# Batched A·Bᵀ on one core: ScalarE and VectorE put into hardware loops, transposes of a and b taken in turn, GpSimd counting landed loads

## The chip, the cores and the metric

One core of one Trainium2 chip. The metric is the device time of one execution in microseconds (us); several executions are taken, and the profiled execution gives the trace. All runs compared here are of the fast state unless a sentence says otherwise. A ratio is the mean time of one kernel's fast runs over the mean time of the other's fast runs in the same rounds, so it is not quite the ratio of the medians quoted next to it. PE is TensorE, DVE is VectorE, ACT is ScalarE, POOL is GpSimd, SP is SyncE.

## The reference

```python
batch, m, k, n = 16, 512, 512, 512          # a: (16,512,512) f32, b: (16,512,512) f32
def reference(a, b):
    return np.matmul(a, b.transpose(0, 2, 1)).astype(np.float32)
```

That is 33.55 MB to read and 16.78 MB to write.

## The kernel before

The 16 products are done as 8 pairs. For each pair SyncE loads 2 MB of a and 2 MB of b; VectorE casts them to bf16 in two halves of the columns (`ha`, `wa`, `hb`, `wb`); PE transposes `ha` and `hb` into PSUM (groups 0 and 1), VectorE copies `wa` over `ha` and `wb` over `hb`, PE transposes those (groups 2 and 3). ScalarE evicts the transposed a to `ta`, VectorE the transposed b to `tb`. Then PE runs 32 matmuls into four PSUM banks, ScalarE copies each result to `ob`, and stores of 1 MB leave. Seven buffers hold loads, seven hold outputs. I call the time from the first transpose of a pair to its first matmul a **turn**, and the 32 matmuls a **block**.

```python
ORDER = "LLLLLLLSLLLLSLSSLSLSLLSSSSSSSSS"     # SyncE: loads and stores; store 0 goes from ScalarE
...
for u in range(pairs):                         # VectorE, unrolled
    ...                                        # casts of a and b, each after its own load
    for ko in range(KO):
        if ko < 2:
            h, w, s_c, s_t = both[ko]
            nc.vector.wait_ge(s_cd, 2 * u + ko + 1)
            nc.vector.wait_ge(s_t, KO * u + 2)
            nc.vector.tensor_copy(out=h[:], in_=w[:]).then_inc(s_c, 1)
        nc.vector.wait_ge(s_tb, KO * u + ko + 1)
        nc.vector.tensor_copy(out=tb[:, ko, :], in_=tp[:, 2 + ko % 2]...).then_inc(s_eb, 1)
...
for x, (h, s_c, s_t, s_e) in enumerate(...):   # PE: a, then b
    take(s_c, 1)
    for g in range(2):
        take(s_e, 1)
        for j in range(2 * J):
            t = nc.tensor.transpose(tp[:, 2 * x + g, j, :], h[:, j, g * P:(g + 1) * P], ident[:])
        t.then_inc(s_t, 1)
```

PE was in a hardware loop already. The waits in its loop have constant counts, while the totals grow with the pair, so there a wait is a `take`: wait for n, then subtract n. In the profile a take is an instruction of the engine's sequencer (51 ns on PE; after the change 21 ns on VectorE and 17 ns on ScalarE); PEq, DVEq or ACTq with the take's line (L186 before, L136 after) as the end of an idle time means that the take was what came last.

Of the kernel before, what the change touches and what calls it, by code (L numbers as in the profile page):

```python
# [10 lines left out]
def kernel(  # L11
# [6 lines left out]
    nc = tc.nc  # L18
    P = 128
    batch, M, K = a.shape  # L20
    _, N, _ = b.shape
    J = M // P
    KO = K // P
    HP = P // 2
    HK = K // 2
    pairs = batch // 2
    f32 = mybir.dt.float32
    bf16 = mybir.dt.bfloat16
    NL = 7
    NO = 7  # L30


    ORDER = "LLLLLLLSLLLLSLSSLSLSLLSSSSSSSSS"

    def sbuf(name, shape, dtype):
        return ctx.enter_context(nc.sbuf_tensor(name, shape, dtype))

    def sem(name):
        return tc.alloc_semaphore(name)

    with tc.tile_critical(no_gpsimd_drain=True):  # L41
        ident = sbuf("ident", [P, P], bf16)
        ld = [sbuf(f"ld{i}", [P, 2 * J, K], f32) for i in range(NL)]
        ha, wa, hb, wb = (
            sbuf(name, [P, 2 * J, HK], bf16) for name in ("ha", "wa", "hb", "wb")
        )
        ta = sbuf("ta", [P, KO, 2 * J * P], bf16)
        tb = sbuf("tb", [P, KO, 2 * J * P], bf16)
        ob = [sbuf(f"ob{i}", [P, J, N], f32) for i in range(NO)]
        tp = ctx.enter_context(nc.psum_tensor("tp", [P, 4, 2 * J, P], bf16))  # L50
        ps = ctx.enter_context(nc.psum_tensor("ps", [P, 4, N], f32))

# [1 line left out]
        s_ld = [sem(f"s_ld{i}") for i in range(NL)]  # L54
        s_second = [sem(f"s_second{i}") for i in range(2)]
        s_st = [sem(f"s_st{i}") for i in range(NO)]
        s_cd = sem("s_cd")
        s_ca = sem("s_ca")
        s_cb = sem("s_cb")
        s_ta = sem("s_ta")  # L60
        s_tb = sem("s_tb")
        s_ea = sem("s_ea")
        s_eb = sem("s_eb")
        s_mm = sem("s_mm")
        s_pv = sem("s_pv")
        s_out = sem("s_out")
# [10 lines left out]



        n_ld, n_st = 0, 1  # L80
        for what in ORDER:
            if what == "L":
                u, slot = n_ld // 2, n_ld % NL
                src = (a if n_ld % 2 == 0 else b)[2 * u:2 * u + 2].rearrange(
                    "e (p j) k -> (e p) j k", j=2 * J
                )
                if n_ld >= NL:

                    nc.sync.wait_ge(s_cd, n_ld - NL + 1)
                if n_ld < 2:  # L90
                    nc.sync.dma_start(
                        ld[slot][:, :J, :], src[:, :J, :]
                    ).then_inc(s_ld[slot], 16)
                    nc.sync.dma_start(
                        ld[slot][:, J:, :], src[:, J:, :]
                    ).then_inc(s_second[slot], 16)
                else:
                    nc.sync.dma_start(ld[slot][:], src).then_inc(s_ld[slot], 16)
                n_ld += 1
            else:  # L100
                slot = n_st % NO
                nc.sync.wait_ge(s_out, n_st + 1)
                nc.sync.dma_start(
                    out[n_st].rearrange("(p j) n -> p j n", j=J), ob[slot][:]
                ).then_inc(s_st[slot], 16)
                n_st += 1
        for n in range(batch - NO, batch - 1):
            nc.sync.wait_ge(s_st[n % NO], 16 * (n // NO + 1))




        nc.vector.nop().then_inc(s_eb, 2)
        nc.vector.wait_ge(s_set, 2)
        both = ((ha, wa, s_ca, s_ta), (hb, wb, s_cb, s_tb))
        for u in range(pairs):
            for x, (h, w, s_c, s_t) in enumerate(both):
                n = 2 * u + x
                src = ld[n % NL]
                nc.vector.wait_ge(s_ld[n % NL], 16 * (n // NL + 1))  # L120
                nc.vector.wait_ge(s_t, KO * u)
                if n >= 2:
                    nc.vector.tensor_copy(out=h[:], in_=src[:, :, :HK]).then_inc(s_c, 1)  # L123
                    nc.vector.tensor_copy(out=w[:], in_=src[:, :, HK:]).then_inc(s_cd, 1)  # L124
                else:
                    nc.vector.tensor_copy(out=h[:, :J, :], in_=src[:, :J, :HK])  # L126
                    nc.vector.tensor_copy(out=w[:, :J, :], in_=src[:, :J, HK:])  # L127
                    nc.vector.wait_ge(s_second[n], 16)
                    nc.vector.tensor_copy(  # L129
                        out=h[:, J:, :], in_=src[:, J:, :HK]  # L130
                    ).then_inc(s_c, 1)
                    nc.vector.tensor_copy(  # L132
                        out=w[:, J:, :], in_=src[:, J:, HK:]
                    ).then_inc(s_cd, 1)
            for ko in range(KO):
                if ko < 2:  # L136
                    h, w, s_c, s_t = both[ko]
                    nc.vector.wait_ge(s_cd, 2 * u + ko + 1)
                    nc.vector.wait_ge(s_t, KO * u + 2)
                    nc.vector.tensor_copy(out=h[:], in_=w[:]).then_inc(s_c, 1)  # L140
                nc.vector.wait_ge(s_tb, KO * u + ko + 1)
                nc.vector.tensor_copy(  # L142
                    out=tb[:, ko, :],
                    in_=tp[:, 2 + ko % 2].rearrange("k j p -> k (j p)"),
                ).then_inc(s_eb, 1)


        nc.scalar.nop().then_inc(s_ea, 2)
        for u in range(pairs):
            for ko in range(KO):  # L150

                nc.scalar.wait_ge(s_ta, KO * u + ko + 1)
                for e in range(2):
                    c = nc.scalar.copy(  # L154
                        out=ta[:, ko, e * J * P:(e + 1) * J * P].rearrange(
                            "k (j p h) -> k j p h", j=J, h=2
                        ),
                        in_=tp[:, ko % 2, :, e * HP:(e + 1) * HP].rearrange(
                            "k (h j) p -> k j p h", h=2
                        ),  # L160
                    )
                c.then_inc(s_ea, 1)
            for e in range(2):
                i = 2 * u + e
                if i >= NO:
                    nc.scalar.wait_ge(s_st[i % NO], 16 * (i // NO))
                for j in range(J):
                    nc.scalar.wait_ge(s_mm, J * i + j + 1)

                    c = nc.scalar.copy(  # L170
                        out=ob[i % NO][:, j, :].rearrange("m (p j) -> m p j", j=2 * J),
                        in_=ps[:, j, :].rearrange("m (j p) -> m p j", j=2 * J),
                    )
                    if j == J - 1:
                        c.then_inc(s_out, 1)
                    elif e == 0 or j == 0:
                        c.then_inc(s_pv, 1)
                    if i == 1 and j == 0:
                        nc.scalar.wait_ge(s_out, 1)
                        nc.scalar.dma_start(  # L180
                            out[0].rearrange("(p j) n -> p j n", j=J), ob[0][:]
                        ).then_inc(s_st[0], 16)


        def take(s, n):
            nc.tensor.wait_ge(s, n).then_inc(s, -n)  # L186

        pe = nc.tensor.engine
        with nc.Fori(0, pairs, engines=[pe]):
            with nc.Fori(0, 2, engines=[pe]):  # L190

                for x, (h, s_c, s_t, s_e) in enumerate(
                    ((ha, s_ca, s_ta, s_ea), (hb, s_cb, s_tb, s_eb))
                ):
                    take(s_c, 1)
                    for g in range(2):
                        take(s_e, 1)
                        for j in range(2 * J):
                            t = nc.tensor.transpose(  # L199
                                tp[:, 2 * x + g, j, :], h[:, j, g * P:(g + 1) * P], ident[:]  # L200
                            )
                        t.then_inc(s_t, 1)
            nc.tensor.wait_ge(s_ea, 2)
            nc.tensor.wait_ge(s_eb, 2)


            for e in range(2):
                for j in range(J):
                    if e == 1 and j % 2 == 0:
                        take(s_pv, 2)  # L210
                    for ko in range(KO):
                        t = nc.tensor.matmul(  # L212
                            ps[:, j, :],
                            ta[:, ko, (e * J + j) * P:(e * J + j + 1) * P],
                            tb[:, ko, :].rearrange("k (j p) -> k j p", j=2 * J)[
                                :, :, e * HP:(e + 1) * HP
                            ],
                            start=(ko == 0),
                            stop=(ko == KO - 1),
                        )  # L220
                    t.then_inc(s_mm, 1)
# [34 lines left out]
```

## Time and profile before

| | before |
|---|---|
| time, median of the first 3 runs | 126.25 us (126.08 to 126.59) |
| span of the profiled run | 124.3 us |
| busy share PE, DVE, ACT | 74%, 55%, 57% |
| DMA | near 100% from 3 to 120 us, mostly 420 to 450 GB/s |
| first block starts, last block starts | 20.59, 107.62 us |

The important part is how the end hangs on the last store and what slack compute has. Beside the slices and windows that the prediction shows, two rows of before matter: from the DMA view the last store's issue to landing (last column, us), and from the view of tile `ld` the range of the loads.

```profile
out_dram<-ob SPq DMA_DIRECT2D x1, 1024.0 KB, 7.6
...
DMA to landing us min/median/max: 5.1/26.0/37.5
```

The last store takes 7.6 us although it is 1 MB, because other stores stand in front of it: the one before it, issued at 111.88, takes 8.6 us itself, and after the change the last store meets an empty queue and takes 3.9 us. That queue is the slack: as long as it is not empty when the last store arrives, compute may be later at little or no cost (in order_only below the last store leaves 2.1 us later, and the ratio is 1.0016, 0.9969 to 1.0063).

### The profile page before, as it was taken

What the parts mean: (1) busy time and instruction counts of PE and PEld (TensorE: products, weight loads), DVE (VectorE), ACT (ScalarE), POOL (GpSimd) and SP (SyncE); (2) the same over time, 40 slices, a digit from 0 to 9 for tenths busy, and PEclk for the clock granted to TensorE, in tenths of its full rate; (3) what the DMA queues carried; (4) which work ended last, traced back from release to release, by engine and by line L of the source; (5) the groups of instructions that cost most, each with busy time, mean ns of one, the idle gap of its engine ahead of it and who ended that gap; (6) DMA issues with size and microseconds to landing.
All of it is one profiled execution on the core that took longest, in us unless ns stands there. A gap on an engine that the chain in (4) does not pass through costs nothing. (4 is left out here: it accounts for less than half of the span.)

```text
span 124.3 us, 2076 instructions
## 1 busy us (share of the span) xinstructions
PE 91.8 (74%) x768; PEld 56.5 (45%) x768; DVE 67.9 (55%) x84; ACT 71.0 (57%) x129; POOL 0.7 (1%) x6
## 2 busy tenths in 40 slices
PE   0005397998699869986998699869986998699000
PEld 0005394447444744574447444744474447443000
DVE  0065668827891788278907890782686568400000
ACT  4006042769476946694669476947694769476100
POOL 2000000000000000000000000000000000000000
PEclk9999999999999999999999999999999999999955
DMA  3999999999999999999999999999999999999980
GB/s 79 403 427 451 443 427 427 427 427 374 411 427 424 445 432 443 424 422 430 414 430 406 416 451 387 403 451 416 448 427 422 419 422 427 427 427 427 424 377 34
DMA packets 4898, 50.35 MB, mean 405 GB/s; under 512 B 544, under 2 KB 544, under 8 KB 544
## 3 DMA queue, kind: packets, MB, share of 16 engines
q1 hardware_dynamic: 4752, 49.29, 94.5%
q10 hardware_dynamic: 144, 1.05, 2.0%
q14 instruction: 2, 0.02, 0.0%
HBM read 33.55 MB, written 16.78 MB: 405 GB/s over the span
## 5 line engine op out<-in xcount | busy, mean ns | idle before, releaser
L212 PE MATMUL ps<-tb,ta 128*128 128x512 bf16 x256 | 57.3, 379 | 8.0 <-DVE tb L142 8.0
L170 ACT COPY ob<-ps 128x512 f32<-128x512 f32 x64 | 37.6, 587 | 30.1 <-PE ps L212 30.1
L212 PEld LDWEIGHTS ps<-tb,ta 128*128 128x128 bf16 x256 | 23.9, 97 | 39.0 <-ACT ta L154 8.2
L154 ACT COPY ta<-tp 128x512 bf16<-128x512 bf16 x64 | 32.9, 604 | 13.3 <-PE tp L199 12.9
L199 PE MATMUL tp<-ident,ha 128*128 128x128 bf16 x256 | 19.7, 230 | 11.8 <-PEq L186 10.9
L199 PEld LDWEIGHTS tp<-ident,ha 128*128 128x128 bf16 x256 | 16.7, 104 | 15.5 <-issue 13.8
L142 DVE COPY tb<-tp 128x1024 bf16<-128x1024 bf16 x32 | 21.3, 685 | 3.9 <-PE tp L199 3.6
L199 PE MATMUL tp<-ident,hb 128*128 128x128 bf16 x256 | 18.5, 230 | 3.1 <-PEq L186 3.1
L199 PEld LDWEIGHTS tp<-ident,hb 128*128 128x128 bf16 x256 | 16.3, 104 | 3.4 <-issue 3.3
L140 DVE COPY ha<-wa 128x2048 bf16<-128x2048 bf16 x8 | 5.5, 693 | 18.1 <-PE tp L199 18.1
L123 DVE CAST hb<-ld 128x2048 bf16<-128x2048 f32 x7 | 8.6, 1226 | 7.2 <-DMA ld<-in_b_dram 7.2
L123 DVE CAST ha<-ld 128x2048 bf16<-128x2048 f32 x7 | 8.5, 1219 | 0.6 <-DMA ld<-in_a_dram 0.6
L124 DVE CAST wb<-ld 128x2048 bf16<-128x2048 f32 x7 | 8.5, 1221 | 0.0
L124 DVE CAST wa<-ld 128x2048 bf16<-128x2048 f32 x7 | 8.5, 1220 | 0.0
L140 DVE COPY hb<-wb 128x2048 bf16<-128x2048 bf16 x8 | 5.5, 685 | 0.2 <-PE tp L199 0.2
L126 DVE CAST ha<-ld 128x1024 bf16<-128x1024 f32 x1 | 0.7, 694 | 6.1 <-DMA ld<-in_a_dram 6.1
L154 ACT ACT_TABLE_LOAD x1 | 1.3, 1283 | 1.0 <-SPq L41 1.0
L129 DVE CAST hb<-ld 128x1024 bf16<-128x1024 f32 x1 | 0.7, 694 | 1.2 <-DMA ld<-in_b_dram 1.2
L126 DVE CAST hb<-ld 128x1024 bf16<-128x1024 f32 x1 | 0.7, 695 | 1.2 <-DMA ld<-in_b_dram 1.2
L129 DVE CAST ha<-ld 128x1024 bf16<-128x1024 f32 x1 | 0.7, 694 | 1.1 <-DMA ld<-in_a_dram 1.1
L132 DVE CAST wa<-ld 128x1024 bf16<-128x1024 f32 x1 | 0.7, 689 | 0.0
L127 DVE CAST wa<-ld 128x1024 bf16<-128x1024 f32 x1 | 0.7, 687 | 0.0
(8 smaller groups left out, 2.3 us busy)
## 6 DMA issues: line engine op xcount, KB each, us to landing
out_dram<-ob SPq DMA_DIRECT2D x15, 1024.0 KB, 25.8
ld<-in_a_dram SPq DMA_DIRECT2D x7, 2048.0 KB, 30.8
ld<-in_b_dram SPq DMA_DIRECT2D x7, 2048.0 KB, 30.5
ld<-in_a_dram SPq DMA_DIRECT2D x2, 1024.0 KB, 6.1
ld<-in_b_dram SPq DMA_DIRECT2D x2, 1024.0 KB, 10.1
out_dram<-ob ACTq DMA_DIRECT2D x1, 1024.0 KB, 12.2
```

What stands on the lines that cost most here:

```text
L123: nc.vector.tensor_copy(out=h[:], in_=src[:, :, :HK]).then_inc(s_c, 1)
L124: nc.vector.tensor_copy(out=w[:], in_=src[:, :, HK:]).then_inc(s_cd, 1)
L126: nc.vector.tensor_copy(out=h[:, :J, :], in_=src[:, :J, :HK])
L127: nc.vector.tensor_copy(out=w[:, :J, :], in_=src[:, :J, HK:])
L129: nc.vector.tensor_copy(out=h[:, J:, :], in_=src[:, J:, :HK]).then_inc(s_c, 1)
L132: nc.vector.tensor_copy(out=w[:, J:, :], in_=src[:, J:, HK:]).then_inc(s_cd, 1)
L140: nc.vector.tensor_copy(out=h[:], in_=w[:]).then_inc(s_c, 1)
L142: nc.vector.tensor_copy(out=tb[:, ko, :], in_=tp[:, 2 + ko % 2].rearrange("k j p -> k (j p)"),).then_inc(s_eb, 1)
L154: c = nc.scalar.copy(out=ta[:, ko, e * J * P:(e + 1) * J * P].rearrange("k (j p h) -> k j p h", j=J, h=2), in_=tp[:, ko % 2, :, e * HP:(e ...
L170: c = nc.scalar.copy(out=ob[i % NO][:, j, :].rearrange("m (p j) -> m p j", j=2 * J), in_=ps[:, j, :].rearrange("m (j p) -> m p j", j=2 * J),)
L199: t = nc.tensor.transpose(tp[:, 2 * x + g, j, :], h[:, j, g * P:(g + 1) * P], ident[:])
L212: t = nc.tensor.matmul(ps[:, j, :], ta[:, ko, (e * J + j) * P:(e * J + j + 1) * P], tb[:, ko, :].rearrange("k (j p) -> k j p", j=2 * J)[:, ...
```

## The change

The intent: a shorter program. ScalarE and VectorE run 8 passes of a loop instead of 8 unrolled copies. That forces other edits: addresses of `ld` and `ob` come from registers, waits become takes, and since the loads rotate over seven DMA semaphores while a wait in the loop names one, GpSimd waits for them in order and passes them on as counts (`s_go`, `s_of`). In the same change PE takes the groups as a, b, a, b; VectorE evicts the first b group before it copies `wa`; casts go by halves of a load; and store 0 moves from ScalarE's queue to SyncE's.

```diff
-    ORDER = "LLLLLLLSLLLLSLSSLSLSLLSSSSSSSSS"
+    ORDER = "LLLLLLLSSLLLLSLSSLSLSLLSSSSSSSSS"
...
+                got = nc.gpsimd.wait_ge(s_ld[n_ld % NL], 16 * (n_ld // NL + 1))
...
+        with nc.Fori(0, pairs, engines=[dve]) as u:
...
+                src = ld[:, bass.ds((u * 2 + x) % NL, 1)].rearrange("p o j k -> p (o j) k")
+                take(s_go, 1)
...
             for ko in range(KO):
-                if ko < 2:
-                    ...                        # copy of w to h, ahead of the eviction
-                nc.vector.wait_ge(s_tb, KO * u + ko + 1)
+                take(s_tb, 1)
+                if ko == 1:
+                    take(s_wb, 1)
+                    nc.vector.tensor_copy(out=hb[:], in_=wb[:]).then_inc(s_cb, 1)
                 nc.vector.tensor_copy(out=tb[:, ko, :], in_=tp[:, 2 + ko % 2]...).then_inc(s_eb, 1)
+                if ko == 0:
+                    take(s_wa, 1)
+                    take(s_da, 1)
+                    nc.vector.tensor_copy(out=ha[:], in_=wa[:]).then_inc(s_ca, 1)
...
+        with nc.Fori(0, pairs, engines=[act]) as u:
...
+                dst = ob[:, bass.ds((u * 2 + e) % NO, 1)].rearrange("m o j n -> m (o j) n")
...
-                for x, (h, s_c, s_t, s_e) in enumerate(
-                    ((ha, s_ca, s_ta, s_ea), (hb, s_cb, s_tb, s_eb))
-                ):
-                    take(s_c, 1)
-                    for g in range(2):
+                for g in range(2):
+                    for x, (h, s_c, s_t, s_e) in enumerate(
+                        ((ha, s_ca, s_ta, s_ea), (hb, s_cb, s_tb, s_eb))
+                    ):
+                        if g == 0:
+                            take(s_c, 1)
```

More of the change, by code (lines that the diff above doesn't have):

```diff
@@ L42 @@
         ident = sbuf("ident", [P, P], bf16)
-        ld = [sbuf(f"ld{i}", [P, 2 * J, K], f32) for i in range(NL)]
+        one = sbuf("one", [P, 1], f32)
+        ld = sbuf("ld", [P, NL, 2 * J, K], f32)
         ha, wa, hb, wb = (
@@ L48 @@
         tb = sbuf("tb", [P, KO, 2 * J * P], bf16)
-        ob = [sbuf(f"ob{i}", [P, J, N], f32) for i in range(NO)]
+        ob = sbuf("ob", [P, NO, J, N], f32)
         tp = ctx.enter_context(nc.psum_tensor("tp", [P, 4, 2 * J, P], bf16))
@@ L56 @@
         s_st = [sem(f"s_st{i}") for i in range(NO)]
+        s_go = sem("s_go")
+        s_of = sem("s_of")
         s_cd = sem("s_cd")
+        s_wa = sem("s_wa")
+        s_wb = sem("s_wb")
         s_ca = sem("s_ca")
         s_cb = sem("s_cb")
+        s_da = sem("s_da")
         s_ta = sem("s_ta")
@@ L74 @@
         ).then_inc(s_set, 1)
-        n_ld, n_st = 0, 1
+        n_ld = n_st = 0
         for what in ORDER:
@@ L87 @@
                 if n_ld >= NL:
-                    nc.sync.wait_ge(s_cd, n_ld - NL + 1)
+                    nc.sync.wait_ge(s_cd, n_ld - NL + 2)
                 if n_ld < 2:
                     nc.sync.dma_start(
-                        ld[slot][:, :J, :], src[:, :J, :]
+                        ld[:, slot, :J, :], src[:, :J, :]
                     ).then_inc(s_ld[slot], 16)
                     nc.sync.dma_start(
-                        ld[slot][:, J:, :], src[:, J:, :]
+                        ld[:, slot, J:, :], src[:, J:, :]
                     ).then_inc(s_second[slot], 16)
                 else:
-                    nc.sync.dma_start(ld[slot][:], src).then_inc(s_ld[slot], 16)
+                    nc.sync.dma_start(ld[:, slot], src).then_inc(s_ld[slot], 16)
                 n_ld += 1
@@ L103 @@
                 nc.sync.dma_start(
-                    out[n_st].rearrange("(p j) n -> p j n", j=J), ob[slot][:]
+                    out[n_st].rearrange("(p j) n -> p j n", j=J), ob[:, slot]
                 ).then_inc(s_st[slot], 16)
@@ L108 @@
             nc.sync.wait_ge(s_st[n % NO], 16 * (n // NO + 1))
+        n_ld = n_st = 0
+        for what in ORDER:
+            if what == "L":
+                got = nc.gpsimd.wait_ge(s_ld[n_ld % NL], 16 * (n_ld // NL + 1))
+                if n_ld < 2:
+                    got.then_inc(s_go, 1)
+                    nc.gpsimd.wait_ge(s_second[n_ld], 16).then_inc(s_go, 1)
+                else:
+                    got.then_inc(s_go, 2)
+                n_ld += 1
+            else:
+                if n_st < batch - NO:
+                    nc.gpsimd.wait_ge(
+                        s_st[n_st % NO], 16 * (n_st // NO + 1)
+                    ).then_inc(s_of, 1)
+                n_st += 1
@@ L113, with taker @@
+        def taker(engine):
+            return lambda s, n: engine.wait_ge(s, n).then_inc(s, -n)
+        dve = nc.vector.engine
+        take = taker(nc.vector)
         nc.vector.nop().then_inc(s_eb, 2)
+        nc.vector.nop().then_inc(s_da, 1)
         nc.vector.wait_ge(s_set, 2)
-        both = ((ha, wa, s_ca, s_ta), (hb, wb, s_cb, s_tb))
-        for u in range(pairs):
-            for x, (h, w, s_c, s_t) in enumerate(both):
-                n = 2 * u + x
-                src = ld[n % NL]
-                nc.vector.wait_ge(s_ld[n % NL], 16 * (n // NL + 1))
-                nc.vector.wait_ge(s_t, KO * u)
-                if n >= 2:
-                    nc.vector.tensor_copy(out=h[:], in_=src[:, :, :HK]).then_inc(s_c, 1)
-                    nc.vector.tensor_copy(out=w[:], in_=src[:, :, HK:]).then_inc(s_cd, 1)
-                else:
-                    nc.vector.tensor_copy(out=h[:, :J, :], in_=src[:, :J, :HK])
-                    nc.vector.tensor_copy(out=w[:, :J, :], in_=src[:, :J, HK:])
-                    nc.vector.wait_ge(s_second[n], 16)
-                    nc.vector.tensor_copy(
-                        out=h[:, J:, :], in_=src[:, J:, :HK]
-                    ).then_inc(s_c, 1)
-                    nc.vector.tensor_copy(
-                        out=w[:, J:, :], in_=src[:, J:, HK:]
-                    ).then_inc(s_cd, 1)
-            for ko in range(KO):
-                if ko < 2:
-                    h, w, s_c, s_t = both[ko]
-                    nc.vector.wait_ge(s_cd, 2 * u + ko + 1)
-                    nc.vector.wait_ge(s_t, KO * u + 2)
-                    nc.vector.tensor_copy(out=h[:], in_=w[:]).then_inc(s_c, 1)
-                nc.vector.wait_ge(s_tb, KO * u + ko + 1)
@@ new lines @@
+        with nc.Fori(0, pairs, engines=[dve]) as u:
+            for x, (h, w, s_c, s_w) in enumerate(
+                ((ha, wa, s_ca, s_wa), (hb, wb, s_cb, s_wb))
+            ):
+                src = ld[:, bass.ds((u * 2 + x) % NL, 1)].rearrange("p o j k -> p (o j) k")
+                take(s_go, 1)
+                if x == 0:
+                    take(s_da, 1)
+                nc.vector.tensor_copy(
+                    out=h[:, :J, :], in_=src[:, :J, :HK]
+                ).then_inc(s_cd, 1)
+                nc.vector.tensor_copy(out=w[:, :J, :], in_=src[:, :J, HK:])
+                take(s_go, 1)
+                nc.vector.tensor_copy(
+                    out=h[:, J:, :], in_=src[:, J:, :HK]
+                ).then_inc(s_c, 1)
+                nc.vector.tensor_copy(
+                    out=w[:, J:, :], in_=src[:, J:, HK:]
+                ).then_inc(s_w, 1)
+            for ko in range(KO):
+                take(s_tb, 1)
+                if ko == 1:
+                    take(s_wb, 1)
+                    nc.vector.tensor_copy(out=hb[:], in_=wb[:]).then_inc(s_cb, 1)
@@ L145 @@
                 ).then_inc(s_eb, 1)
+                if ko == 0:
+                    take(s_wa, 1)
+                    take(s_da, 1)
+                    nc.vector.tensor_copy(out=ha[:], in_=wa[:]).then_inc(s_ca, 1)
+        act = nc.scalar.engine
+        take = taker(nc.scalar)
         nc.scalar.nop().then_inc(s_ea, 2)
-        for u in range(pairs):
+        nc.scalar.nop().then_inc(s_of, NO)
+        nc.scalar.copy(out=one[:], in_=nc.const_aps.tensor(1.0, (P, 1), f32))
+        with nc.Fori(0, pairs, engines=[act]) as u:
             for ko in range(KO):
-                nc.scalar.wait_ge(s_ta, KO * u + ko + 1)
+                if ko < KO - 1:
+                    nc.scalar.wait_ge(s_ta, ko + 1)
+                else:
+                    take(s_ta, KO)
                 for e in range(2):
@@ L162 @@
                 c.then_inc(s_ea, 1)
+            take(s_of, 2)
             for e in range(2):
-                i = 2 * u + e
-                if i >= NO:
-                    nc.scalar.wait_ge(s_st[i % NO], 16 * (i // NO))
+                dst = ob[:, bass.ds((u * 2 + e) % NO, 1)].rearrange("m o j n -> m (o j) n")
                 for j in range(J):
-                    nc.scalar.wait_ge(s_mm, J * i + j + 1)
+                    if j < J - 1:
+                        nc.scalar.wait_ge(s_mm, j + 1)
+                    else:
+                        take(s_mm, J)
                     c = nc.scalar.copy(
-                        out=ob[i % NO][:, j, :].rearrange("m (p j) -> m p j", j=2 * J),
+                        out=dst[:, j, :].rearrange("m (p j) -> m p j", j=2 * J),
                         in_=ps[:, j, :].rearrange("m (j p) -> m p j", j=2 * J),
@@ L177 @@
                         c.then_inc(s_pv, 1)
-                    if i == 1 and j == 0:
-                        nc.scalar.wait_ge(s_out, 1)
-                        nc.scalar.dma_start(
-                            out[0].rearrange("(p j) n -> p j n", j=J), ob[0][:]
-                        ).then_inc(s_st[0], 16)
-        def take(s, n):
-            nc.tensor.wait_ge(s, n).then_inc(s, -n)
         pe = nc.tensor.engine
+        take = taker(nc.tensor)
         with nc.Fori(0, pairs, engines=[pe]):
             with nc.Fori(0, 2, engines=[pe]):
-                for x, (h, s_c, s_t, s_e) in enumerate(
-                    ((ha, s_ca, s_ta, s_ea), (hb, s_cb, s_tb, s_eb))
-                ):
-                    take(s_c, 1)
-                    for g in range(2):
+                for g in range(2):
+                    for x, (h, s_c, s_t, s_e) in enumerate(
+                        ((ha, s_ca, s_ta, s_ea), (hb, s_cb, s_tb, s_eb))
+                    ):
+                        if g == 0:
+                            take(s_c, 1)
                         take(s_e, 1)
@@ L201 @@
                             )
+                            if x == 1 and g == 1 and j == 0:
+                                t.then_inc(s_da, 1)
                         t.then_inc(s_t, 1)
```

## The prediction

> **What bounds the kernel now.** I read the 40 slices first, because they say whether anything is busy without a pause.
>
> ```profile
> PE   0005397998699869986998699869986998699000
> DVE  0065668827891788278907890782686568400000
> ACT  4006042769476946694669476947694769476100
> DMA  3999999999999999999999999999999999999980
> GB/s 79 403 427 451 443 427 427 427 427 374 411 427 424 445 432 443 424 422 430 414 430 406 416 451 387 403 451 416 448 427 422 419 422 427 427 427 427 424 377 34
> ```
>
> The DMA row is 9 from the second slice to the last but two. PE, DVE and ACT all have dips in a four-slice rhythm. So the transfers are the bound: 50.33 MB (33.55 read, 16.78 written) at the 427 GB/s of most slices take 118 us. Around them lie the start (first issue at 0.94 us, queues full from about 3 us) and the end.
>
> The chain of what ended last holds only 7% PE and 1% DVE, so it is no help here: it breaks off in the middle of the matrix work, while the end waits on stores. The views that help are the windows and the issues at the tail.
>
> ```profile
> 110.00:116.00 6.00, 4.80 (x22) 1.88 (x20) 0.00 (x0) 3.65 (x7) 0.00 (x0) 1.00 1.01 425
> 116.00:118.00 2.00, 0.00 (x0) 0.00 (x0) 0.00 (x0) 0.00 (x0) 0.00 (x0) 1.00 1.02 430
> 119.00:120.00 1.00, 0.00 (x0) 0.00 (x0) 0.00 (x0) 0.00 (x0) 0.00 (x0) 0.50 0.99 418
> 121.00:122.00 1.00, 0.00 (x0) 0.00 (x0) 0.00 (x0) 0.00 (x0) 0.00 (x0) 0.50 0.33 139
> ...
> 114.84 0.59 ACT L170 COPY ob<-ps 128x512 f32<-128x512 f32 x1 [0.28 <-PE ps L212]
> 115.45 0.33 SPq L103 DMA_DIRECT2D out_dram<-ob  x1
> ```
>
> The two last columns of a window are the DMA share and GB/s. Compute is over at 115.43, yet the DMA engines stay full until about 120. The last store is issued at 115.45 and its issue row gives 7.6 us to landing, so it lands at 123.05; the span ends 1.25 us later. A 1 MB transfer that meets an empty queue needs less: the very first one takes 5.1 us from issue to landing (the least of the 5.1/26.0/37.5 us of the loads). So the last store could be issued at 123.05 - 5.1 = 117.95 without moving the end. Compute has a slack of **2.5 us** over the whole program, and nothing is to be gained by finishing it sooner.
>
> Compute itself is a second, almost equal bound, with its own rhythm: the timeline has the matmul blocks starting at 20.59 and 107.62, so (107.62 - 20.59)/7 = 12.43 us a pair. It doesn't wait for loads: the largest DMA wait of a cast after the start is 3.3 us, and it ends before PE is free. One turn between two blocks looks so:
>
> ```profile
> 102.19 1.06 PE L199 MATMUL tp<-ident,ha 128*128 128x128 bf16 x16
> 102.87 4.17 ACT L154 COPY ta<-tp 128x512 bf16<-128x512 bf16 x8
> 103.08 1.06 PE L199 MATMUL tp<-ident,hb 128*128 128x128 bf16 x16
> 103.35 0.69 DVE L140 COPY ha<-wa 128x2048 bf16<-128x2048 bf16 x1 [0.51 <-PE tp L199]
> 104.34 1.34 PE L199 MATMUL tp<-ident,ha 128*128 128x128 bf16 x16 [0.20 <-PEq L186]
> 106.19 1.29 DVE L142 COPY tb<-tp 128x1024 bf16<-128x1024 bf16 x2 [0.34 <-PE tp L199]
> 107.62 7.18 PE L212 MATMUL ps<-tb,ta 128*128 128x512 bf16 x32 [1.02 <-DVE tb L142]
> ```
>
> From the first transpose to the matmul block 5.43 us pass. The last tb eviction ends at 107.48 and the block starts 0.14 us later: DVE's chain ends the turn, ACT's ta evictions (done at 107.04) are close behind.
>
> [...]the ScalarE store of before agrees: issued at 25.11 it took 12.2 us, while the slices stayed near 427. So moving it to SyncE gains no bandwidth. [...]PE already loops in the kernel before, and its restarts inside a turn cost 0.20 us (the row "PEq L186" above)[...]. [...]
>
> **The change, part by part.**
>
> *Transfers.* Same 34 DMAs, same bytes. Store 0 goes to SyncE's queue; the order of the rest is kept. Load n now waits for the first half cast of load n-6 instead of the last cast of load n-7. I checked each against the timeline: only load 10 is held, from 30.44 to about 33.4 (cast of load 4 at 32.76). By then loads 0 to 9 and two stores, 23 MB, are queued, enough until about 2.6 + 23/0.427 = 56 us. Cost: 0. Full-length transfer time: unchanged.
>
> *Loops and registers.* DVE gets 8 fused register instructions per pair, one ahead of each half cast, and ACT 8, one ahead of each output copy. [...]my guess is 0.1 to 0.3 us each. On DVE they lie in the cast phase, which has 3.1 to 3.8 us of idle ahead of the copy of wa when no load is late. On ACT they sit in the 0.28 us between two copies (copies of 0.587 us, period 0.87 us); at worst the last copy of a pair slips by 0.2 us. [...]Sum on the path: 0.2 us at the end of the program.
>
> *Half casts.* Two whole casts spaced 1.14 us become four halves spaced 0.61 us (first pair's rows: 6.11 then 6.72), so 2.44 against 2.28 us per tensor: 0.3 us more per pair, in DVE's idle time. Cost 0.
>
> *GpSimd as a relay.* One more semaphore hop between landing and cast, guessed 0.1 to 0.2 us. On the path once, for the first b: 0.15 us, and with its register work 0.25 us.
>
> *The order of transposes, start.* Before, both a groups are transposed at 9.51, while b is still coming. Now the second a group stands behind the first b group, which starts at 14.48 + 0.25. Seven groups of 8 then have to follow, not six: PE is cold there (1.87 us for 16, so about 0.85 a group), and DVE's copies of wa and wb wait for later groups. Walking through the waits I get b1 done at 17.4, the copy of wb at 18.2, the last b group at 21.15, its eviction at 21.95, the matmul block at 22.1 instead of 20.59. Loss 1.0 to 1.5 us, the lower figure if PE warms up on the way.
>
> *The order of transposes, each turn.* With a turn's first transpose at 0 and a group every 0.445 us: b0 is done at 1.06, tb0 is evicted 1.17-1.85, wa copied 1.77-2.46, wb 2.37-3.05, tb1 evicted 2.97-3.65. PE takes a2 at 2.66 (before at 2.15), b2 at 3.25, a3 at 3.70, b3 at 4.14, done 4.75; tb3 is evicted 4.86-5.54 and the block starts at 5.69, against 5.43 before. That is 0.25 us for each of 7 turns, 1.75 us; DVE starts useful evictions sooner, but the copies that PE waits for move back behind them.
>
> *Sum.* Compute ends later by 1.25 + 1.75, together about 3.0 us, plus 0.2 for ACT: the last store is issued at about 118.6. Slack 2.5 us, so the end moves by about **0.6 us**: 126.25 + 0.6 = 126.8 (rounded down[...]).
>
> **Rivals.** (1) *Nothing moves*: the turns are as fast as before or faster, since tb0's eviction no longer waits for the second a group and ACT's evictions, not DVE's, may end the turn. For it speaks the 100% DMA row; then compute is late by under 2.5 us and the time is 126.0 to 126.5. About as likely as my sum. (2) *Register work or loop branches are slow*: if a register instruction takes over 0.3 us, ACT's copy period passes 0.87 us, or a branch stalls the turn by 1 us. Then 8 us of compute are added and the slack eats 2.5: 130 us or more. Against it speak the short loops. (3) *A gain*: one ring instead of two removes the slice of 374 GB/s near 29 us, when ScalarE's store and the loads share the engines. One slice of 3.1 us at 374 instead of 427 is 0.4 us[...]. At most 125.8 us.
>
> **Range and chances.** The transfers set a floor near 125.8. Compute can be 2.5 us late for free and my estimate of its lateness is 3 us, give or take 1.6. So 8 times in 10 between 125.8 and 128.4. Over 2% faster would need 123.7, below the floor of the transfers: 0.02. Over 2% slower means over 128.8, so compute late by 5 us: 0.09. Within 2%: 0.89.
>
> **What would show it.** Right: the DMA row still 9 throughout; first matmul block near 22; blocks 12.5 to 12.8 us apart; last output copy ending at 117.5 to 119.5; the last store landing 5 us after its issue instead of 7.6. Wrong: gaps in the DMA row before 118 us (a load that waited for a slot); ACT output copies over 0.87 us apart with "issue" ahead of them (slow registers); turns shorter than 5.4 us (the new order helps, the time stays); blocks over 13 us apart, which the slack can't carry.

## The result, and the profile after

The changed kernel takes 127.44 us (127.32 to 127.73, 4 runs) against 126.4 us for the kernel before; the ratio is 1.0088, 95% interval 1.0059 to 1.0118. That is 0.9% slower, clear of noise and within 2%.

The slices of the changed kernel, 3.1 us each:

```profile
PE   0003386997699769996899769976997699769900
DVE  0066487926794479537971898089817891750000
DMA  4999999999999999999999999999999999999764
GB/s 86 399 433 433 439 423 439 428 439 428 423 324 428 459 392 433 423 433 433 407 459 392 407 454 386 407 459 415 441 423 423 420 425 428 420 428 397 321 264 164
```

Compute now runs to the end of the program and the DMA row ends in 7, 6, 4 instead of 9, 8, 0: the transfers waited for compute at the end. There is also one slice of 324 GB/s near 36 us that the kernel before doesn't have. The windows of the tail (last columns DMA share and GB/s), the last output copy and store, and that store's issue to landing:

```profile
116.00:118.00 2.00, 1.96 (x10) 0.74 (x9) 0.00 (x0) 1.45 (x3) 0.00 (x0) 1.00 0.60 250
118.00:120.00 2.00, 1.53 (x8) 0.49 (x5) 0.00 (x0) 1.16 (x3) 0.00 (x0) 1.00 0.95 393
120.00:121.00 1.00, 0.00 (x0) 0.00 (x0) 0.00 (x0) 0.31 (x1) 0.00 (x0) 1.00 0.09 33
121.00:123.00 2.00, 0.00 (x0) 0.00 (x0) 0.00 (x0) 0.00 (x0) 0.00 (x0) 1.00 0.96 393
...
119.73 0.58 ACT L212 COPY ob<-ps 128x512 f32 x1 [0.35 <-ACTq L136]
...
120.34 0.33 SPq L110 DMA_DIRECT2D out_dram<-ob  x1
...
out_dram<-ob SPq DMA_DIRECT2D x1, 1024.0 KB, 3.9
```

The DMA engines stand at 0.09 between 120 and 121 us: nothing is left to move until the last store is issued at 120.34. It meets an empty queue and lands 3.9 us later, and the program ends 1.25 us after that: 120.34 + 3.9 + 1.25 = 125.5, which is the span. So compute is 120.34 - 115.45 = 4.89 us later, and 1.2 us of it shows (span 125.5 against 124.3). The slow slice near 36 us can't be what ends this kernel: the engines have long caught up when they run dry (0.60 busy from 116 to 118 us, 0.09 from 120 to 121).

Where the 4.89 us come from: the first block starts at 21.18 instead of 20.59 (+0.59); the blocks are (112.26 - 21.18)/7 = 13.01 us apart instead of 12.43 (+0.58 in each of 7 periods, +4.05); the rest, from the last block's start to the last store, is 8.08 instead of 7.83 us (+0.25). One turn after the change, to be laid beside the one that the prediction shows:

```profile
106.34 0.61 PE L235 MATMUL tp<-ident,ha 128*128 128x128 bf16 x8
106.78 0.61 PE L235 MATMUL tp<-ident,hb 128*128 128x128 bf16 x8
...
107.54 0.69 DVE L171 COPY tb<-tp 128x1024 bf16<-128x1024 bf16 x1 [3.50 <-DVEq L136]
...
108.15 0.68 DVE L178 COPY ha<-wa 128x2048 bf16<-128x2048 bf16 x1
108.75 0.69 DVE L170 COPY hb<-wb 128x2048 bf16<-128x2048 bf16 x1
...
109.13 0.61 PE L235 MATMUL tp<-ident,ha 128*128 128x128 bf16 x8 [0.84 <-PEq L136]
...
111.42 0.69 DVE L171 COPY tb<-tp 128x1024 bf16<-128x1024 bf16 x1 [0.20 <-DVEq L136]
...
112.26 7.27 PE L250 MATMUL ps<-tb,ta 128*128 128x512 bf16 x32 [0.98 <-DVE tb L171]
```

The turn is 112.26 - 106.34 = 5.92 us against 5.43. The copy of `wa` starts 1.81 us into the turn (1.16 before) since an eviction stands ahead of it, and the third a group 2.79 (2.15 before). The block lasts until the next turn begins: 99.23 to 106.34, 7.11 us, against 70.26 to 77.28, 7.02 us before. Together 0.49 + 0.09 = 0.58 us a pair. (Single turns and blocks vary a little: the turns after alternate between 5.92 and 5.88 us, and the first three blocks before last 6.97. The periods average over this.)

### The profile page after: what moved, and what is told of

It is laid out like the page before. It is cut to its first block, busy times and chain, and to the rows that moved or that the text cites. A ratio compares the mean times of both kernels' runs of the same rounds, so it can differ in the third digit from the quotient of the medians.

```text
span 125.5 us, 2399 instructions
## 1 busy us (share of the span) xinstructions
PE 91.2 (73%) x768; PEld 55.1 (44%) x768; DVE 70.8 (56%) x112; ACT 71.9 (57%) x130; POOL 0.7 (1%) x6
## 5 line engine op out<-in xcount | busy, mean ns | idle before, releaser
L212 ACT COPY ob<-ps 128x512 f32 x64 | 37.5, 585 | 28.9 <-PE ps L250 23.2
L194 ACT COPY ta<-tp 128x512 bf16<-128x512 bf16 x64 | 33.7, 599 | 18.5 <-PE tp L235 17.9
L171 DVE COPY tb<-tp 128x1024 bf16<-128x1024 bf16 x32 | 22.1, 690 | 30.1 <-DVEq L136 30.1
L235 PE MATMUL tp<-ident,ha 128*128 128x128 bf16 x256 | 20.7, 227 | 16.0 <-PEq L136 16.0
L235 PE MATMUL tp<-ident,hb 128*128 128x128 bf16 x256 | 20.3, 225 | 4.1 <-PEq L136 4.0
L155 DVE CAST ha<-ld 128x1024 bf16 x8 | 5.6, 694 | 6.8 <-DVEq L136 6.4
L155 DVE CAST hb<-ld 128x1024 bf16 x8 | 5.5, 690 | 1.7 <-DVEq L136 1.7
L160 DVE CAST hb<-ld 128x1024 bf16 x8 | 5.5, 689 | 1.1 <-DVEq L136 1.1
L160 DVE CAST ha<-ld 128x1024 bf16 x8 | 5.5, 687 | 1.0 <-DVEq L136 1.0
L163 DVE CAST wb<-ld 128x1024 bf16 x8 | 5.5, 688 | 0.0
L158 DVE CAST wb<-ld 128x1024 bf16 x8 | 5.5, 688 | 0.0
L163 DVE CAST wa<-ld 128x1024 bf16 x8 | 5.5, 688 | 0.0
L158 DVE CAST wa<-ld 128x1024 bf16 x8 | 5.5, 686 | 0.0
```

Source lines behind the costliest of these rows:

```text
L155: nc.vector.tensor_copy(out=h[:, :J, :], in_=src[:, :J, :HK]).then_inc(s_cd, 1)
L158: nc.vector.tensor_copy(out=w[:, :J, :], in_=src[:, :J, HK:])
L160: nc.vector.tensor_copy(out=h[:, J:, :], in_=src[:, J:, :HK]).then_inc(s_c, 1)
L163: nc.vector.tensor_copy(out=w[:, J:, :], in_=src[:, J:, HK:]).then_inc(s_w, 1)
L194: c = nc.scalar.copy(out=ta[:, ko, e * J * P:(e + 1) * J * P].rearrange("k (j p h) -> k j p h", j=J, h=2), in_=tp[:, ko % 2, :, e * HP:(e ...
L212: c = nc.scalar.copy(out=dst[:, j, :].rearrange("m (p j) -> m p j", j=2 * J), in_=ps[:, j, :].rearrange("m (j p) -> m p j", j=2 * J),)
```

## The experiments

Three theories for the 4.89 us and the 0.9%: (1) the new order makes each turn longer; (2) the loops do, by registers, takes, branches or the relay; (3) the transfers themselves got slower, by the single store queue. Each run below says what each expected.

**order_back**: the changed kernel with the old order.

```diff
-                for g in range(2):
-                    for x, ... in enumerate(...):
+                for x, ... in enumerate(...):
+                    for g in range(2):
...
+                if ko == 0:                    # wa copied ahead of the eviction again
+                    take(s_wa, 1); take(s_da, 1)
+                    nc.vector.tensor_copy(out=ha[:], in_=wa[:]).then_inc(s_ca, 1)
                 take(s_tb, 1)
```

> The changed kernel with its loops, registers, relay and single store queue, but with the old order (PE a a b b, VectorE copies wa before the first tb eviction). Theory 1 (the new order makes each turn 0.5 us longer; registers only cost about 0.1 us a pair): turns of 5.4 us again, blocks 12.5 us apart, last output copy ends near 116.6, so the last store is issued inside the slack (limit about 119.0) and the time is 126.3 to 126.6. Theory 2 (registers, branches and relay make the turns long): blocks stay 13.0 us apart and the time stays at 127.4. Theory 3 (the single store queue loses 0.6 us of transfer near 37 us): compute as in theory 1, but the time is 126.9 to 127.1.

126.88 us against 126.4 (ratio 1.0043, 1.0003 to 1.0083). That time is about what theory 3 expected, and two_rings below tests it. The blocks start at 20.25 and 109.82: 12.80 us apart, neither the 12.5 of theory 1 nor the 13.0 of theory 2. The order accounts for 0.22 us a pair and the loops for the other 0.36 (12.80 - 12.43). Rows of its trace for a turn (first transpose at 78.54) show what starts later:

```profile
78.90 0.59 ACT L212 COPY ob<-ps 128x512 f32 x1 [0.35 <-ACTq L136]
...
79.80 0.69 DVE L170 COPY ha<-wa 128x2048 bf16<-128x2048 bf16 x1 [3.70 <-DVEq L136]
...
84.23 1.02 PE L250 MATMUL ps<-tb,ta 128*128 128x512 bf16 x4 [1.14 <-DVE tb L175]
```

The last output copy begins 0.36 us into the turn, where the kernel before has 0.20 (77.48 after 77.28), and the copy of `wa` at 1.26 instead of 1.16. The turn is 84.23 - 78.54 = 5.69 us with the old order: 0.26 us of loop cost lie in the turn and 0.09 in the block (7.11 against 7.02; 0.14 against before's first three blocks).

**order_only**: the kernel before, unrolled, with only the new order on PE and VectorE (the same two blocks of the diff above, with the old waits).

> The kernel before (unrolled, no relay, store 0 from ScalarE) with only the new order on PE and VectorE. Theory 1: turns of 5.85 us, blocks 12.87 us apart, first block near 21.0, last block near 111.1, last store issued near 119.1, just at the end of the slack: 126.3 to 126.8. Theory 2: blocks 12.43 us apart as before, time 126.3.

126.43 us against 126.4 (1.0016, 0.9969 to 1.0063; one of six runs at 127.83). Its turn goes from 78.59 to the block at 84.29, 5.70 us, against 5.43; the turns alternate between 5.70 and 5.66, the blocks are as long as before, and the period is (109.70 - 20.91)/7 = 12.68 us, so the order costs 0.25 us a pair. Its last store leaves at 117.53, 2.1 us later than before, and lands 5.6 us later at 123.1: compute later by 2 us, no time lost. Both theories 1 and 2 hold: of the 0.58 us a pair the order makes 0.22 to 0.25 and the loops 0.36.

**one_ring**: the kernel before with store 0 on SyncE's queue.

```diff
-    ORDER = "LLLLLLLSLLLLSLSSLSLSLLSSSSSSSSS"
+    ORDER = "LLLLLLLSSLLLLSLSSLSLSLLSSSSSSSSS"
-        n_ld, n_st = 0, 1
+        n_ld = n_st = 0
...
-                        nc.scalar.dma_start(out[0]..., ob[0][:]).then_inc(s_st[0], 16)
```

> The kernel before, with only store 0 moved from ScalarE's queue to SyncE's, ahead of store 1. Theory 3 (two stores in a row on the loads' queue lose transfer time): a dip of the DMA share to about 0.7 for 2 us near 37 us, all later landings 0.5 to 0.7 us later, time 126.9 to 127.1. Otherwise: no dip that the kernel before doesn't have, time 126.3.

126.84 us against 126.4, but the runs fall apart in two groups (126.18 to 126.44 and 127.24 to 127.58) and the ratio is 1.0020, 0.9977 to 1.0064: unresolved. The profiled run, 127.28, is of the slower group. The dip itself is there. The window of 36 to 38 us, first of one_ring and then of the kernel before:

```profile
36.00:38.00 2.00, 2.00 (x11) 0.81 (x9) 1.30 (x2) 1.45 (x3) 0.00 (x0) 1.00 0.77 250
```

```profile
36.00:38.00 2.00, 2.00 (x11) 0.87 (x9) 1.67 (x2) 1.45 (x3) 0.00 (x0) 1.00 0.98 418
```

The load that lands next after the dip lands at 49.39 instead of 48.06, and the last store, issued at 115.94, at 124.19 instead of 123.02: in this profiled run the delay is of the kind that was expected, and larger (1.3 and 1.2 us instead of 0.5 to 0.7).

**act_unrolled**: the changed kernel with ScalarE unrolled and constant addresses, takes kept.

```diff
-        with nc.Fori(0, pairs, engines=[act]) as u:
+        for u in range(pairs):
...
-                dst = ob[:, bass.ds((u * 2 + e) % NO, 1)].rearrange("m o j n -> m (o j) n")
+                dst = ob[:, (u * 2 + e) % NO]
```

> The changed kernel with ScalarE's loop unrolled again (constant addresses, everything else as changed). If the register instruction ahead of an output copy costs 0.09 us and reaches PE through the release of the PSUM banks: matmul blocks 7.02 us again instead of 7.11, period 12.92 instead of 13.01, last store 0.7 us earlier, time 127.4 - 0.7 = 126.7. If ScalarE's registers cost nothing on the path: 127.4.

127.03 us against 126.4 (1.0037, 1.0004 to 1.0070). Blocks start at 22.04 and 112.16, 12.87 us apart: 0.14 us a pair belongs to ScalarE's loop. The first output copy starts 1.06 us after the block (74.59 after 73.53) instead of the 1.20 of the changed kernel. So it is the registers and not the branch: the branch lies behind the last output copy, and the delay is there at the first. The view of that line in the changed kernel has the register instruction:
```profile
L212 ACTq FUSED_REGOPS  x64: 46/46/117, 22.2 to 119.6; - x64
```

There are 64, one ahead of each output copy, of 46 to 117 ns (min/median/max). The first one starts at 22.2 us, 0.2 us before its copy at 22.39, though ScalarE had been idle since 20.94 (the start of the first block is 21.18): it waits for PE too, so it isn't done ahead of time. The turn is 5.92 us as changed (80.50 to 86.42), and the block is 6.97 us instead of 7.11 (73.53 to 80.50): the whole 0.14 us lies in the block, where PE waits for released copies before it writes the banks again. The last store left at 120.03, hardly earlier, because the first block of this profiled run started late: a group of 8 transposes took 0.97 to 1.06 us up to the one at 19.64 us, and 0.61 us only from 20.44 us on. More on that below. It also landed 4.43 us after its issue, not 3.9.

**late3** and **late8**: the kernel before with idle work ahead of the first copies, to measure what lateness costs by itself.

```diff
+            if u == 0:
+                for n in range(3):             # 8 in late8
+                    nc.vector.memset(junk[:], 0.0).then_inc(s_junk, 1)
+                    nc.vector.wait_ge(s_junk, n + 1)
             for ko in range(KO):
```

> The kernel before with 3 idle VectorE memsets (1024 elements, with a wait between) ahead of the first pair's copies: compute starts later by L, read as last store issue minus 115.45 us, and nothing else changes. L should be 2 to 3.6 us, inside the slack of 3.6 us that the changed kernel's last store (3.9 us from issue to landing) implies: time 126.3 to 126.6. If the slack were only the 2.5 us of the prediction, the time would be L - 2.5 us longer.

> As late3 with 8 memsets: L of 5.5 to 9.5 us, beyond the slack. The time should be 126.4 + (L - 3.6), within 0.5 us; the DMA share should have a gap ahead of the last store. If compute were not what the end hangs on, the time would stay 126.4.

late3: 127.8 us (1.0092, 1.0050 to 1.0134). Its lateness is not the 2 to 3.6 us that I wanted but 5.70 us (last store at 121.15): PE ran the whole first round of transposes slowly (1.86 to 1.91 us for 16, where 1.06 is usual later) and its first block took 9.39 us instead of 7.13. With its measured lateness it fits what is worked out below: 121.15 + 3.9 + 1.25 = 126.3, its span. late8: 131.72 us (1.0408, 1.0358 to 1.0458, three fast runs of four), last store at 124.80, lateness 9.35, and 124.80 + 3.9 + 1.25 = 129.95, its span being 130.0. Two windows of late8 show the empty queue ahead of the last stores:

```profile
117.00:118.00 1.00, 1.00 (x5) 0.45 (x6) 0.00 (x0) 0.00 (x0) 0.00 (x0) 1.00 0.16 66
118.00:124.00 6.00, 6.00 (x28) 2.47 (x26) 0.00 (x0) 4.10 (x7) 0.00 (x0) 1.00 0.34 142
```

So the end is, to a first approximation, the later of two things: the transfers' own end (last landing at 123.05 in the kernel before), and last store + 3.9 us. They meet at 123.05 - 3.9 = 119.15, so the slack is 119.15 - 115.45 = 3.7 us. With it late8 should lose 9.35 - 3.7 = 5.65 us of span and lost 5.7; the changed kernel 4.89 - 3.7 = 1.2 and lost 1.2.

**wa_first**: the changed kernel with VectorE's old order alone.

> The changed kernel with only VectorE's order put back (copy of wa, tb eviction, copy of wb, tb eviction), PE still turning a and b in turn. The copy of wb then stands behind the first tb eviction and reaches PE later: a turn of 6.5 us by the same walk through the waits (5.92 as changed). 0.6 us by 7 turns is 4.2 us more compute, with no slack left: 131 to 132 us. If the order of VectorE were harmless: 127.4.

One fast run, 131.42 us, as expected; three others at 134.18 to 134.51 are classed as slow, and no ratio was formed. The profiled run is one of those. I use of it only the turn, 72.19 to 78.58, 6.39 us, which is the expected effect and a little smaller than the 6.5 of the walk. VectorE's old order under PE's new one is worse than either matched pair; the opposite mixture was not run.

**dve_plain** and **dve_unrolled**: the changed kernel with VectorE unrolled; dve_plain waits on absolute counts, dve_unrolled keeps the takes.

```diff
-        with nc.Fori(0, pairs, engines=[dve]) as u:
+        for u in range(pairs):
...
-                src = ld[:, bass.ds((u * 2 + x) % NL, 1)]...
+                src = ld[:, (u * 2 + x) % NL]
```

and in dve_plain alone

```diff
-        take = taker(nc.vector)
+        def take(s, n):                        # no subtraction: wait for the running total
+            seen[s.name] = seen.get(s.name, 0) + n
+            nc.vector.wait_ge(s, seen[s.name])
```

> The changed kernel with VectorE unrolled and waiting on absolute counts (no registers, no separate take instructions), all else as changed. If the 0.35 us a pair that the loops cost is shared between ScalarE's output copies (0.13 us, measured by act_unrolled) and VectorE's takes ahead of the evictions (0.1 us or more): period 12.8 to 12.9 instead of 13.01 us, last store 0.8 to 1.5 us earlier, time 126.5 to 127.0. If VectorE's loop costs nothing on the path: period 13.0, time 127.4.

> The changed kernel with VectorE unrolled and constant addresses, but still with its separate take instructions. dve_plain took both away and shortened the period by 0.22 us (13.01 to 12.79). If the takes (a wait as an instruction of its own ahead of each eviction) are the cost: period 12.95 to 13.01, time 127.3. If the registers or the loop branch are: 12.8, time 127.0.

dve_plain: 127.01 us (1.0046, 1.0007 to 1.0085), blocks (110.31 - 20.77)/7 = 12.79 us apart. dve_unrolled: 127.46 us (1.0073, 1.0036 to 1.0110), blocks (112.30 - 21.22)/7 = 13.01 us apart, exactly those of the changed kernel. So on VectorE the registers and the loop branch cost nothing on the path, and the takes cost 0.22 us a pair. First the first eviction of a turn of dve_unrolled (first transpose at 80.36), then the first and the last eviction of a turn of dve_plain (first transpose at 79.03) and the block after them:

```profile
81.57 0.69 DVE L171 COPY tb<-tp 128x1024 bf16<-128x1024 bf16 x1 [3.65 <-DVEq L136]
```

```profile
80.12 0.69 DVE L176 COPY tb<-tp 128x1024 bf16<-128x1024 bf16 x1 [3.53 <-PE tp L240]
...
83.89 0.69 DVE L176 COPY tb<-tp 128x1024 bf16<-128x1024 bf16 x1 [0.20 <-PE tp L240]
...
84.73 3.61 PE L255 MATMUL ps<-tb,ta 128*128 128x512 bf16 x16 [0.88 <-ACT ta L199]
```

In dve_plain the first eviction starts 1.09 us into the turn instead of 1.20, the last 4.86 instead of 5.08, and the block 5.70 instead of 5.92. The packed trace of dve_unrolled has the take as a 21 ns instruction of VectorE's sequencer, and where the eviction waits for it, the eviction starts 0.106 to 0.108 us after the take does. In dve_plain no instruction stands ahead of these evictions. dve_plain removed two things at once, the separate instruction and its subtraction. The kernel before has a separate wait without a subtraction ahead of its copies of `wa`; there the copy starts 0.065 us after it. So the separate instruction seems to be the larger part; no run changes the one without the other.

**two_rings**: order_back with store 0 back on ScalarE's queue (ScalarE's first pair peeled off the loop).

> The changed kernel with loops and relay, the old order, and store 0 back on ScalarE's queue (ScalarE's first pair is peeled off its loop for that). Compute as in order_back (last store near 117.9 us, inside the slack). If the single queue is what keeps order_back at 126.9: no dip near 37 us, last landing 123.1 instead of 123.5, time 126.3 to 126.5. If something else of the changed kernel does it: 126.9.

127.14 us against 126.63 in its rounds (1.0045, 1.0013 to 1.0078): no better than order_back's 1.0043. The dip is gone (36 to 38 us: DMA share 1.01, 430 GB/s), the last store left at 118.50 and landed 4.9 us later at 123.4. The single queue is not what keeps order_back above the kernel before. By chance this run repeats act_unrolled's result within one program: the first pair, peeled off and with constant addresses, has a block of 6.97 us, those in the loop 7.11 (as has the first pair of the changed kernel).

**apart**: one_ring with two loads between stores 0 and 1.

```diff
-    ORDER = "LLLLLLLSSLLLLSLSSLSLSLLSSSSSSSSS"
+    ORDER = "LLLLLLLSLLSLLSLSSLSLSLLSSSSSSSSS"
```

> one_ring with two loads between store 0 and store 1. If the dip comes from two stores in a row behind the loads, it is halved or gone here, and the time is 126.4; if it comes from the first store on that queue behind a load, the dip near 37 us stays and the time is about that of one_ring, 126.8.

126.87 us (1.0030, 0.9990 to 1.0070). The dip stays (36 to 38 us: share 0.79, 270 GB/s), so it doesn't need two stores in a row.

**two_starts**: the kernel before, with the first b loaded from ScalarE's queue.

```diff
-                    nc.sync.dma_start(
+                    q = nc.sync if n_ld == 0 else nc.scalar
+                    q.dma_start(
```

> An attempt to beat both: the kernel before with the first b's two loads issued from ScalarE's queue, so that the DMA engines fill up sooner than 3 us. They stand at 0.18 and 0.74 busy in the second and third microsecond; filled at once, at most 0.4 us of transfer is gained: 126.0. If the two queues only share what one had: 126.4.

126.44 us against 126.63 (0.9979, 0.9943 to 1.0015). The third microsecond fills from 0.74 to 0.92, the fourth falls from 0.99 to 0.88. PE begins only at 14.45 us instead of 9.51, and the first block at 21.58 instead of 20.59. A gain isn't shown. No version here is clearly faster than the kernel before, and by its DMA row (near 100% from 3 to 120 us of a span of 124.3) none that moves the same bytes can be by much.

## Why the prediction came out as it did

The time (126.8 predicted, 127.44 measured) was in the range and the sign was right. The structure held: transfers bound the kernel, compute has a slack, the change makes compute later by more than the slack, and only the excess counts. Its terms, in order:

- **Order, each turn: 0.25 us predicted, 0.25 measured** (order_only, period 12.68 against 12.43; its turns are 5.70 and 5.66, the walk had said 5.69). The walk through the waits was right as a walk: its steps lie within 0.08 us of the turn of order_only that begins at 78.59. So was the cause: VectorE's copies of `wa` and `wb`, on which PE waits, moved behind an eviction.
- **Loops and registers: "Sum on the path: 0.2 us at the end of the program". This is the step that failed.** The runs show 0.36 us in every pair (order_back 12.80 against 12.43), so 2.5 us over seven periods: on VectorE 0.22 us by the takes (dve_plain against dve_unrolled), on ScalarE 0.14 us by the registers ahead of its output copies (act_unrolled). Both were measured under the new order, and they add up to the 0.36 of the old one; with the order's 0.22 (13.01 less 12.80) they make 0.58. The prediction looked for the price of the register instructions, and on VectorE, where there are eight a pair, they are free as it said (13.01 us a pair with them and, in dve_unrolled, without); it didn't price the takes at all. It had two of them before its eyes and misread them: it takes the 0.20 us of the row "PEq L186" for a loop's restart, but L186 is the take. In the packed trace of that turn PE's loop branch (L190) is over at 103.30, and the 0.20 us end with two takes at 104.08 and 104.23, after the copy of `wa` that ended at 104.04. The branch itself is recorded with 76 to 226 ns on PE in the kernel before, and after the change with 40 to 50 ns on ScalarE and 50 to 63 ns on VectorE. On ScalarE it let the last copy of a pair slip by 0.2 us "at worst" and took that to matter once, while PE's wait for released PSUM banks brings the slip back in every block.
- **Start: 1.0 to 1.5 us predicted, 0.59 measured.** The prediction left open whether PE would get faster on the way, and it did: a group of 8 transposes takes 1.00 to 1.06 us up to the one at 17.83 us and 0.61 us from 18.69 us on, and in an unbroken row groups start 0.86 us apart before (15.52, 16.38) and 0.44 to 0.45 after (18.69, 19.13, 19.58). The trace's clock record begins, at full clock, at 18.69 us too. In the kernel before PE transposed without a pause from 14.48 us, and the record begins, at full clock, at 19.55, 5.1 us later; the 16 transposes at 17.84 still took 1.87 us. When PE gets faster differs from run to run: the first group of 0.61 us is the one at 17.87 us in dve_unrolled and the one at 20.44 in act_unrolled, and in late3 16 transposes at 21.14 still took 1.91 us and the first block, from 23.93 us, 9.39 us. What sets that moment was not tested. The first block of the profiled runs thus starts anywhere from 20.25 to 22.04 us in kernels that differ little at the start, and a part of the scatter of the times may come from there; I didn't test that.
- **Slack: 2.5 us predicted, 3.7 measured.** The term was mis-sized because 5.1 us, from the first load, stood in for a store that meets an empty queue, which takes 3.9 us (after, late3, late8). Why the first load took longer was not tested; other loads were queued behind it, and the DMA share was still 0.18 and 0.74 in the second and third microsecond.
- **Sum.** Predicted lateness 3.2, slack 2.5, excess 0.6. Measured 4.89 - 3.7 = 1.2. Two errors of more than a microsecond, the loops and the slack, went in opposite directions, and the start helped, so the total looks better than its parts.
- **GpSimd's relay**: 0.15 us predicted, 0.25 with the register work; both were guesses, not read from a trace. The first cast begins at 6.41 instead of 6.11 and the first b's at 11.26 instead of 11.00; their second halves come 0.20 later. From landing to cast the first b takes 0.02 us in before, 0.07 in dve_plain (relay alone), 0.18 in dve_unrolled (relay and takes) and 0.34 in the changed kernel. So the relay is 0.05 us, the take 0.11 and the register work 0.16 of 0.32 us.
- **Transfers "unchanged"**: load 10 was held, until 34.84 us (33.4 worked out). The dip near 37 us was not foreseen; it doesn't come from that hold, since one_ring has the dip and doesn't hold the load. In bytes it is worth (418 - 250) x 2 us / 427 = 0.8 us. The landings agree: the next load after it lands 0.8 us later in order_back than in two_rings (49.54 against 48.76). By the load that lands near 82 us this pair is level again (81.65 and 81.61), while one_ring is still late at its end; each is one profiled execution, and the rounds of one_ring and two_rings don't resolve any cost in time. So its cause and its price at the end stay open. It appears in all eight kernels with store 0 on SyncE's queue (302 to 332 GB/s in the 12th of the 40 slices, near 36 us) and in none of the six with store 0 on ScalarE's (399 to 439).
- **Rivals.** The first fails by the turns, 5.92 us instead of 5.43 or less. The second had the right place, but the register instructions, 46 to 126 ns, stay below its 0.3 us, and no branch stalled a turn by 1 us. The third was right that the slice of 374 GB/s near 29 us goes (428 after), and missed that one of 324 comes near 36. The same slice is an exception to the prediction's "the slices stayed near 427".

Of the signs named in advance for "right", the short time to landing of the last store (3.9 us; 5 named) and the first block near 22 (21.18) came; "the DMA row still 9 throughout", "blocks 12.5 to 12.8 us apart" and "last output copy ending at 117.5 to 119.5" didn't (13.01, 120.31). Of those for "wrong", two came: blocks over 13 us apart, which the slack didn't carry, and a gap in the DMA row before 118 us (0.60 from 116), here by late stores and not by a load.

The slack's edge is soft. order_back, two_rings and dve_plain issued their last stores 1.25, 0.65 and 0.76 us inside the slack and still measured 0.4 to 0.5% above the kernel before. Their traces show that the DMA engines partly ran dry all the same. One window of the kernel before, then of two_rings:

```profile
118.00:119.00 1.00, 0.00 (x0) 0.00 (x0) 0.00 (x0) 0.00 (x0) 0.00 (x0) 0.77 1.01 426
```

```profile
118.00:119.00 1.00, 0.00 (x0) 0.00 (x0) 0.00 (x0) 0.48 (x1) 0.00 (x0) 1.00 0.55 229
```

In order_back the share is 0.80 there, in dve_plain 0.62. Part of it is that a store's bytes don't flow at its issue: in the changed kernel the last one is issued at 120.34, and the share is 0.04 from 120.5 to 121.0. The last landings are at 123.5, 123.4 and 123.7 us instead of 123.0. That fits the 0.4 to 0.5%, but it is one profiled execution of each, order_back and dve_plain have the dip near 37 us too, and no run tests the edge by itself.

## What to carry to other kernels

When transfers fill the whole span, compute first the slack of compute: the last landing, less the time that the last store needs on an empty queue (3.9 us for 1 MB here), less the moment it is issued now. Take it as an upper limit, for the edge is soft: versions 0.65 to 1.25 us inside it lost 0.4 to 0.5% here. Then any change of compute is priced by what it exceeds the slack, and a cost that returns in every pass has to be multiplied before it is compared with it (0.36 us a pair were 2.5 us here). In a hardware loop look first for waits that became instructions of their own ahead of the work that the next engine waits for (0.22 us a pair on VectorE here); the address registers may be free where the engine has idle time in front, as on VectorE here (13.01 us a pair with and without), while on ScalarE they cost 0.14 us a pair.
